# Two token tiles at a stage border: landing order, a two-engine evacuation and constant matmuls

## The chip, the cores and the metric

The kernel runs on one core of a Trainium2 chip. The metric is the device time of one execution in microseconds (us), lower is better. Each time is the median of several runs.

## What is computed

The program chains two blocks of two layers over 256 tokens of width 1024, in float32, and every layer is a mixer followed by a mixture of 16 experts. Between them stand residual additions and layer norms:

```python
h = _layer_norm(x) * (1.0 + sc1) + sh1
mix = _mixer(h, w_in[l], ...)
x = _layer_norm(DN_ALPHA * x + g1 * mix, ln1_g[l], ln1_b[l])
h = _layer_norm(x) * (1.0 + sc2) + sh2
ffn = _moe(h, w_router, router_bias, ...)
x = _layer_norm(DN_ALPHA * x + g2 * ffn, ln2_g[l], ln2_b[l])
```

That is a layer of the first block. In the second block the mixer is a gated linear attention in layer 0 and a differential attention in layer 1, there is no modulation by `sc` and `sh`, and each norm stands behind its addition in the same way.

## The kernel before

The 256 tokens are two token tiles of 128 rows, and both live in one SBUF tile `X` for the whole program. Every float32 product of the mixers is made from high and low parts: `hh` and `hl` of the activations, `whi` and `wlo` of the weights, with three matmuls for each pair (`acc<-whi,hh`, `acc<-whi,hl`, `acc<-wlo,hh`). The high part is a rounding to fp32r, and the low part is what is left of the value.

There are four mixtures in the order of the program, which the code tags `moe10`, `moe11`, `moe20` and `moe21`. This text calls them the first to the fourth. Their last step and the first step of what follows are what the text calls a **border**: border 1 leads from the first mixture into the mixer of layer 1 of the first block (`block1`, line 1116), border 2 from the second into the gated linear attention (`gla`, line 1506), border 3 from the third into the differential attention (`diff`, line 1683), and behind the fourth comes the end of the program (line 1858).

A mixture works through eight pairs of experts, `pi` 0 to 7. At its start the router (lines 541 and 567) makes the chosen experts' mask `r_m`. While PE waits for it, `keep_warm` (lines 702 and 946) issues matmuls of constants into a bank that nobody reads; their number is the third one in `WARM` (line 98). Then five small matmuls (line 704) make the places `pos` of the tokens, DVE turns them into one-hot rows `oh` (line 720), and the matmuls `pg` gather the tokens.

A pair ends with `spread`, which brings the experts' output `y` back to the token tiles (matmuls `sc`, one bank for each token tile and half of the columns), and `land`, which adds it to `X` (line 851). At the last pair `land` also does the norm that follows, through an object of the class `Tail` (line 255): `count` takes the statistics of one half (BN_STATS), `first` closes them (BN_AGGR, `ve` on DVE, then the power `rs` on POOL, line 189), and `affine` applies them in two passes, one with the mean (line 278) and one with `rs` (line 281). In the first block a second set of statistics follows for the norm of the next layer.

The next stage then transposes each token tile on PE (line 300), eight blocks of 128x128 into two banks `pt`, and evacuates them as `hh` and `hl`. At border 1 DVE first normalises (`z`, line 1208), and the evacuation also modulates. For each bank ACT makes three of four blocks and DVE the fourth in float32 (`hf`), then DVE casts all four to `hh` and subtracts for `hl`:

```python
if c < 3:
    S.activation(t[:, c], pt[:, c], AF.Identity, bias=sh1[:, k:k + 1], scale=sc1[:, k:k + 1])
else:
    V.tensor_scalar(t[:, c], pt[:, c], sc1[:, k:k + 1], sh1[:, k:k + 1], op0=OP.mult, op1=OP.add)
V.tensor_copy(hh[dst], t)
V.tensor_tensor(hl[dst], t, hh[dst].bitcast(F32), op=OP.subtract)
```

The order on each engine is settled when the program is built. Around a border (`chain_begins` to `chain_ends`, lines 235 to 249) the order of DVE, POOL, ACT and PE is the one in which the code was written; elsewhere a scheduler sets it. Each engine takes its instructions strictly in that order, and waits at the head of its row for the semaphores of the others.

Of the kernel before, what the change touches and what calls it, by code (L numbers as in the profile page):

```python
# [10 lines left out]
F32 = mybir.dt.float32  # L11
# [3 lines left out]
AF = mybir.ActivationFunctionType  # L15
# [81 lines left out]
TAIL_ENG = (ENG.Activation, ENG.PE)  # L97
WARM = ((3, 2, 6), (3, 2, 6))
LAM_WAIT = 8
# [26 lines left out]
def body(ctx: ExitStack, tc: tile.TileContext, A: dict, out: bass.AP, dbg=None):  # L126
# [135 lines left out]
    class Tail:  # L262
# [7 lines left out]
        def count(self, tt, h):  # L270
            self.stats[tt].add(h, X[:, tt, h * 512:(h + 1) * 512])

        def first(self, tt):
            self.mr[tt] = self.stats[tt].close()

        def affine(self, tt):
            x, (mu, rs) = X[:, tt], self.mr[tt]
            V.scalar_tensor_tensor(x, x, mu, self.rows[:, 0], op0=OP.subtract, op1=OP.mult)
            again = Stats(2)
            for h, hs in enumerate((slice(0, 512), slice(512, 1024))):  # L280
                V.scalar_tensor_tensor(x[:, hs], x[:, hs], rs, self.rows[:, 1, hs], op0=OP.mult, op1=OP.add)  # L281
                if self.again:
                    again.add(h, x[:, hs])
                yield hs
            if self.again:
                self.mr[tt] = again.close()
# [341 lines left out]
    def moe(z, kind, slots, scored, wg, wu, wd, mod, gate, tag, after, again, reorder=False, room=()):  # L628
# [7 lines left out]
        with ExitStack() as es:  # L636
# [167 lines left out]
            def down(pi, st, aT, last=False):  # L804
# [4 lines left out]
                for h in range(2):  # L809
# [19 lines left out]
                    if last and h == 0 and NF > 2:  # L829
                        land(pi, 0, spread(st, yh, yl, 0))  # L830
                if last and NF == 2:
                    land(pi, 0, sc)
                return yh, yl

            def spread(st, yh, yl, h):

                hs = slice(h * 512, (h + 1) * 512)
                scs = []
                for tt in range(2):
                    sc = ps.tile([P, 512], F32, tag="sc", name="sc", bufs=2)  # L840
                    mm3(sc, [(st[:, tt * P:(tt + 1) * P], yy[:, hs]) for yy in (yh, yl)])
                    scs.append(sc)
                return scs

            def land(pi, h, scs):
                hs = slice(h * 512, (h + 1) * 512)
                for tt, sc in enumerate(scs):
                    if pi == 0:
                        V.scalar_tensor_tensor(X[:, tt, hs], X[:, tt, hs], ALPHA, sc, op0=OP.mult, op1=OP.add)
                    else:  # L850
                        V.tensor_tensor(X[:, tt, hs], X[:, tt, hs], sc, op=OP.add)  # L851
                    if pi == 7 and (tt, h) != (1, 1):
                        tail.count(tt, h)
                    if pi == 7 and (tt, h) == (0, 1):
                        tail.first(0)
                        for _ in tail.affine(0):
                            pass

# [67 lines left out]
            for pi in range(8):  # L926
                if pi < 7:
                    if pi % 2 == 1:
                        gx = gather(pi // 2 + 1)
                    gu = up(pi + 1, gx[1])  # L930
                st = ga[0]
                ys = down(pi, *ga, pi == 7)
                if pi < 7:
                    ga = act(pi + 1, gx[0], gx[2], *gu)
                    land(pi, 0, spread(st, *ys, 0))
                land(pi, 1, spread(st, *ys, 1))
                if pi == OV_AT:
                    overflow()
                if pi == 6:
                    tail = Tail(after(), again)  # L940
                    chain_begins(*TAIL_ENG)
            rings[:] = [ring] * RING
            turn[0] = 0
# [172 lines left out]
    def block1(l, prev):  # L1116

        with tc.tile_pool(name="gp", bufs=1, reuse_waits="tile") as gp:
            gates[l, 1] = gp.tile([P, D], F32, name="g2")
            es = gp.tile([P, 2, NE], F32, name="es")  # L1120
            with ExitStack() as stack:
# [67 lines left out]
                def ev(tt, q, pt):  # L1189
                    ts = slice(tt * P, (tt + 1) * P)  # L1190
                    t = dl.tile([P, 4, P], F32, tag="hf", name="hf", bufs=2)
                    for c in range(4):
                        k = 4 * q + c
                        if c < 3:
                            S.activation(t[:, c], pt[:, c], AF.Identity, bias=sh1[:, k:k + 1], scale=sc1[:, k:k + 1])
                        else:
                            V.tensor_scalar(t[:, c], pt[:, c], sc1[:, k:k + 1], sh1[:, k:k + 1], op0=OP.mult, op1=OP.add)
                    dst = (slice(None), slice(4 * q, 4 * q + 4), ts)
                    V.tensor_copy(hh[dst], t)
                    V.tensor_tensor(hl[dst], t, hh[dst].bitcast(F32), op=OP.subtract)  # L1200

                if prev is not None:
                    for tt in range(2):
# [5 lines left out]
                        if tt == 0:  # L1209
                            prev.count(1, 1)  # L1210
                            prev.first(1)
                        prev.lows()
                        transposed(ps, "tp", z[:, tt], tt, ev)
                    chain_ends()
                dump(f"x{l}", X)
# [290 lines left out]
    def gla(prev, gp, room, load_router, logits, rows):  # L1506
        with tc.tile_pool(name="dl", bufs=1, reuse_waits="tile") as dl, tc.tile_pool(name="d", bufs=1, reuse_waits="tile") as d, tc.tile_pool(name="d2", bufs=2, reuse_waits="tile") as d2, \
# [21 lines left out]
            for tt in range(2):  # L1529
                if tt == 0:  # L1530
                    prev.count(1, 1)
                    prev.first(1)
                else:
# [149 lines left out]
    def diff(prev, gp, room, load_router, logits, rows):  # L1683
        with tc.tile_pool(name="dl", bufs=1, reuse_waits="tile") as dl, tc.tile_pool(name="d", bufs=1, reuse_waits="tile") as d, tc.tile_pool(name="d2", bufs=2, reuse_waits="tile") as d2, \
# [24 lines left out]
            for tt in range(2):  # L1709
                if tt == 0:  # L1710
                    prev.count(1, 1)
                    prev.first(1)
                else:
# [139 lines left out]
    ov = out[0].rearrange("(t p) d -> t p d", p=P)  # L1853
    prev.count(1, 1)
    prev.first(1)
    for tt in range(2):
# [40 lines left out]
```

## Time and profile before

| | us |
|---|---|
| median of three runs | 1644.25 (1643.98 to 1645.04) |
| profiled execution, its own time | 1644.99 |
| its span, from the first to the last instruction | 1643.2 |
| PE busy | 1464.9 (89%) |
| DVE busy | 867.5 (53%) |
| ACT busy | 430.3 (26%) |
| POOL busy | 132.9 (8%) |
| mean granted clock of PE | 0.952 of full speed |

A row of a timeline gives the start from the beginning of the span, the duration, the engine and line, the operation with the tile it writes and those it reads, and in square brackets how long the engine was idle before it and who released it. An `x8` behind a row says that eight instructions of one kind stand in it. A line number can be that of a helper. A matmul in float32 has two rows, one in fp32r has one. The granted clock is 1.00 at 2.4 GHz and 0.50 at 1.2 GHz.

### The profile page before, as it was taken

The page shows a single profiled execution, that of the slowest core. Times are in us where ns is not written, and L with a number is a line of the kernel's source. Part 1 is how long each engine was busy: PE and PEld are TensorE (multiplying, and loading weights), DVE is VectorE, ACT ScalarE, POOL GpSimd, SP SyncE. Part 2 cuts the span into 40 slices and gives each one's busy share as a digit, 9 for nine tenths or more (in the row PEclk, how much of TensorE's full clock was granted, in tenths as well). Part 3 has the DMA queues.
Part 4 walks back from the last instruction along what each step waited for, and adds up shares of the span by engine and source line. Part 5 has one row for each costly group of instructions (what it writes and reads, how often), then busy time and mean ns, then how long its engine had stood idle before and what let it go on. Part 6 is the DMA issues. An engine that isn't in the chain of part 4 may idle for free. (4 is left out here: it accounts for less than half of the span.)

```text
span 1643.2 us, 22584 instructions
## 1 busy us (share of the span) xinstructions
PE 1464.9 (89%) x9024; PEld 968.6 (59%) x9024; DVE 867.5 (53%) x1678; ACT 430.3 (26%) x729; POOL 132.9 (8%) x140
## 2 busy tenths in 40 slices
PE   4899997998699999599878998999898999999896
PEld 3788896443288899444447695443336988344332
DVE  3788898343798779524363574221126776122214
ACT  1453341111244433111125242010003552101000
POOL 0300002000130000200020001000002002000000
PEclk9999998999799999799989999999998999999898
DMA  9978699994775688899476387999989856999992
GB/s 307 365 245 282 202 312 352 340 308 165 248 252 171 205 294 251 240 367 358 156 241 199 104 290 256 375 376 366 360 306 296 272 204 240 359 367 387 334 387 104
DMA packets 324383, 461.80 MB, mean 281 GB/s; under 512 B 20077, under 2 KB 178285, under 8 KB 324258
## 3 DMA queue, kind: packets, MB, share of 16 engines
q1 hardware_dynamic: 308400, 445.29, 79.0%
q10 hardware_dynamic: 15858, 14.85, 3.5%
q8 instruction: 77, 1.26, 0.3%
q14 instruction: 48, 0.39, 0.1%
HBM read 456.43 MB, written 3.67 MB: 280 GB/s over the span
## 5 line engine op out<-in xcount | busy, mean ns | idle before, releaser
L763 PE MATMUL gu<-w,xg 128*64 128x512 f32 x1536 | 366.6, 597 | 7.3 <-ACT sa L796 6.5
L763 PEld LDWEIGHTS gu<-w,xg 128*64 128x64 f32 x1536 | 111.2, 137 | 218.9 <-issue 203.1
L817 PE MATMUL y<-w,sa 128*64 128x512 f32 x768 | 207.1, 596 | 1.1 <-DVE sa L801 1.1
L335 DVE TENSOR_TENSOR wlo<-w,whi 128x2048 fp32r<-128x2048 f32 (+2 forms) x92 | 183.4, 1997 | 45.3 <-ACT whi L325 42.4
L325 ACT ACTIVATE whi<-w 128x2048 fp32r<-128x2048 f32 (+2 forms) x92 | 157.7, 1726 | 141.0 <-PE acc L406 103.2
L828 DVE TENSOR_TENSOR yy<-y,yy 128x512 fp32r<-128x512 f32 x32 | 22.1, 692 | 197.3 <-ACT yy L827 197.3
L817 PEld LDWEIGHTS y<-w,sa 128*64 128x64 f32 x768 | 60.9, 137 | 107.4 <-issue 101.0
L501 DVE SCALAR_TENSOR_TENSOR adac<-w,ce,adac 128x512 f32<-128x512 f32 x140 | 104.5, 747 | 1.2
L313 PE MATMUL sc<-yy,st 128*128 128x512 f32 x256 | 87.2, 434 | 19.2 <-ACT yy L827 11.0
L313 PE MATMUL pg<-oh,zh 128*128 128x256 f32 x256 | 77.8, 332 | 25.3 <-DVEq L870 21.7
L406 PE MATMUL acc<-hh,whi 128*128 128x256 f32 x608 | 92.5, 294 | 1.7 <-ACT whi L325 1.7
L406 PE MATMUL acc<-hl,whi 128*128 128x256 f32 x608 | 93.0, 288 | 0.0
L827 ACT ACTIVATE yy<-y 128x512 fp32r<-128x512 f32 x32 | 19.1, 597 | 274.4 <-PE y L817 274.4
L406 PE MATMUL acc<-hh,wlo 128*128 128x256 f32 x608 | 87.1, 282 | 0.2 <-DVE wlo L335 0.2
L851 DVE TENSOR_TENSOR x<-x,sc 128x512 f32<-128x512 f32 x112 | 73.3, 681 | 22.0 <-PE sc L313 21.9
L406 PEld LDWEIGHTS acc<-hh,whi 128*128 128x128 f32 x608 | 80.0, 194 | 7.7 <-issue 4.7
L406 PEld LDWEIGHTS acc<-hl,whi 128*128 128x128 f32 x608 | 80.2, 191 | 4.8 <-issue 4.2
L313 PEld LDWEIGHTS pg<-oh,zh 128*128 128x128 f32 x256 | 58.3, 229 | 39.1 <-PEq L870 18.6
L189 POOL TENSOR_TENSOR rs<-ve,mhalf 128x1 f32<-128x1 f32 x24 | 25.3, 1055 | 678.7 <-DVE ve L188 678.7
L313 PEld LDWEIGHTS sc<-yy,st 128*128 128x128 f32 x256 | 42.0, 188 | 63.5 <-ACT yy L827 26.7
L406 PEld LDWEIGHTS acc<-hh,wlo 128*128 128x128 f32 x608 | 77.8, 188 | 2.2 <-issue 1.7
L823 DVE TENSOR_TENSOR yt<-y,g 128x512 f32<-128x512 f32 x32 | 22.0, 688 | 106.5 <-PE y L817 95.4
(375 smaller groups left out, 2196.9 us busy)
## 6 DMA issues: line engine op xcount, KB each, us to landing
w<-in_moe_w_gate_dram SPq DMA_DIRECT2D x64, 1024.0 KB, 12.1
w<-in_moe_w_up_dram SPq DMA_DIRECT2D x64, 1024.0 KB, 14.3
w<-in_moe_w_down_dram SPq DMA_DIRECT2D x128, 512.0 KB, 10.8
w<-in_w_ada_dram SPq DMA_DIRECT2D x47, 1024.0 KB, 6.5
w<-in_w_in_dram SPq DMA_DIRECT2D x40, 1024.0 KB, 6.6
w<-in_w_exp_gate_dram SPq DMA_DIRECT2D x64, 512.0 KB, 8.7
w<-in_w_exp_up_dram SPq DMA_DIRECT2D x64, 512.0 KB, 8.8
w<-in_w_exp_down_dram SPq DMA_DIRECT2D x64, 512.0 KB, 9.1
```

The source lines that it names most:

```text
L189: G.tensor_tensor(dst, ve, mhalf[:, :n], op=OP.pow)
L313: PE.matmul(dst, l, r, start=(i == 0), stop=(i == n - 1), skip_group_check=True)
L325: S.activation(hi[:, k0:k0 + n], w, AF.Copy)
L335: eng.tensor_tensor(lo[:, k0 + x:k0 + y], w[:, x:y], hi[:, k0 + x:k0 + y].bitcast(F32), op=OP.subtract)
L406: PE.matmul(dst, l, r, start=(start and i == 0), stop=(i == n - 1), skip_group_check=True)
L501: V.scalar_tensor_tensor(acc, ws[k // 4][:, k % 4], ce[:, k:k + 1], acc, op0=OP.mult, op1=OP.add)
L763: PE.matmul(gu[64 * j:64 * j + 64, :], xg[:, 4 * kh + k, (2 * pr + j) * CAP:(2 * pr + j + 1) * CAP], ws[j][:, k, :], start=(kh == 0 and k ...
L817: PE.matmul(y[64 * j:64 * j + 64, :], aT[:, f, 64 * j:64 * j + 64], w[:, j, k, :], start=(f == 0), stop=(f == NF - 1), tile_position=(0, 6 ...
L823: V.tensor_tensor(yt[:, hs], y, gate[:, hs], op=OP.mult)
L827: S.activation(yh[:, hs], src, AF.Copy)
L828: V.tensor_tensor(yl[:, hs], src, yh[:, hs].bitcast(F32), op=OP.subtract)
L851: V.tensor_tensor(X[:, tt, hs], X[:, tt, hs], sc, op=OP.add)
```

## The change

- `WARM`: 12 instead of 8 constant matmuls stand in front of `pos` at the start of each mixture.
- `TAIL_WARM` (new): behind the last `spread` of a mixture stand 14 constant matmuls at the first, 8 at the second and third, none at the fourth. At border 1 three more stand behind the transposes of each token tile.
- `land` is called for one token tile at a time. The first tile's halves land first, and its norm begins; the second tile's first half lands between the two passes of the first tile's `affine`, its second half behind it. `second` takes the statistics of both halves of the second tile, behind the work on the first. The last `spread` writes to banks of another tag (`gu`), so it need not wait for those of the first half.
- Border 1's evacuation: for each of four blocks ACT makes `hh` from `pt`, rounded as it is written, and DVE makes `hf` from the same `pt`. The cast is gone.

```diff
-WARM = ((3, 2, 6), (3, 2, 6))
+WARM = ((3, 2, 10), (3, 2, 10))
+TAIL_WARM = {"moe10": (14, 3), "moe11": (8, 0), "moe20": (8, 0), "moe21": (0, 0)}
...
+        def second(self):
+            for h in range(2):
+                self.count(1, h)
+            self.first(1)
...
-        def affine(self, tt):
+        def affine(self, tt, between=None):
             x, (mu, rs) = X[:, tt], self.mr[tt]
             V.scalar_tensor_tensor(x, x, mu, self.rows[:, 0], op0=OP.subtract, op1=OP.mult)
+            if between is not None:
+                between()
...
+                if last:
+                    if NF == 2:
+                        land(pi, 0, sc[:1])
+                    scs = spread(st, yh, yl, 1, "gu")
+                    land(pi, 1, scs[:1])
+                    tail.first(0)
+                    for _ in tail.affine(0, lambda: land(pi, 0, sc[1:], 1)):
+                        pass
+                    land(pi, 1, scs[1:], 1)
...
+            keep_warm(ps, "tp", 2, TAIL_WARM[tag][0])
...
-                        if c < 3:
-                            S.activation(t[:, c], pt[:, c], AF.Identity, bias=sh1[:, k:k + 1], scale=sc1[:, k:k + 1])
-                        else:
-                            V.tensor_scalar(t[:, c], pt[:, c], sc1[:, k:k + 1], sh1[:, k:k + 1], op0=OP.mult, op1=OP.add)
+                        S.activation(hh[:, k, ts], pt[:, c], AF.Identity, bias=sh1[:, k:k + 1], scale=sc1[:, k:k + 1])
+                        V.tensor_scalar(t[:, c], pt[:, c], sc1[:, k:k + 1], sh1[:, k:k + 1], op0=OP.mult, op1=OP.add)
                     dst = (slice(None), slice(4 * q, 4 * q + 4), ts)
-                    V.tensor_copy(hh[dst], t)
                     V.tensor_tensor(hl[dst], t, hh[dst].bitcast(F32), op=OP.subtract)
...
-                            prev.count(1, 1)
-                            prev.first(1)
+                            prev.second()
                         prev.lows()
                         transposed(ps, "tp", z[:, tt], tt, ev)
+                        keep_warm(ps, "acc", 3, TAIL_WARM["moe10"][1])
```

The same `prev.second()` stands in `gla`, `diff` and at the end of the program.

The first place is PE at border 1: `sc` is the last spread, `pt` the transposes (eight blocks for each token tile), `acc` the products of the mixer of layer 1, of which the first 48 read the first token tile. Before:

```order
L817 MATMUL y<-w,sa 64x512 x6
L313 MATMUL sc<-yy,st 128x512 x8
L300 MATMUL pt<-consts,z 128x128 x8
L406 MATMUL acc<-whi,hh 128x256 x8
L406 MATMUL acc<-whi,hl 128x256 x8
L406 MATMUL acc<-wlo,hh 128x256 x8
L406 MATMUL acc<-whi,hh 128x256 x8
L406 MATMUL acc<-whi,hl 128x256 x8
L300 MATMUL pt<-consts,z 128x128 x8
L406 MATMUL acc<-wlo,hh 128x256 x8
```

Now:

```order
L825 MATMUL y<-w,sa 64x512 x6
L321 MATMUL sc<-yy,st 128x512 x8
L964 MATMUL warm<-consts 128x256 x14
L308 MATMUL pt<-consts,z 128x128 x8
L964 MATMUL warm<-consts 128x256 x3
L308 MATMUL pt<-consts,z 128x128 x8
L964 MATMUL warm<-consts 128x256 x3
L414 MATMUL acc<-whi,hh 128x256 x8
L414 MATMUL acc<-whi,hl 128x256 x8
L414 MATMUL acc<-wlo,hh 128x256 x8
```

The transposes of the second token tile used to stand behind 40 of the 48 products on the first tile. Now no product stands between the transposes of the two tiles: all 48 follow the second tile's, with constant matmuls before each group.

The second place is ACT at border 1, with the engines whose semaphores each instruction waits for (`PE_49`, `DVE_49`); `pt` with four numbers are the four banks of the two token tiles. Before:

```order
L1195 ACTIVATE hf_5419<-pt_5414,modc_83 128x128 [waits PE_49]
L1195 ACTIVATE hf_5419<-pt_5414,modc_83 128x128 x2
L1195 ACTIVATE hf_5431<-pt_5426,modc_83 128x128 [waits PE_49]
L1195 ACTIVATE hf_5431<-pt_5426,modc_83 128x128 x2
L1195 ACTIVATE hf_5460<-pt_5455,modc_83 128x128 [waits DVE_49,PE_49,Activation_49]
L1195 ACTIVATE hf_5460<-pt_5455,modc_83 128x128 x2
L1195 ACTIVATE hf_5472<-pt_5467,modc_83 128x128 [waits DVE_49,PE_49,Activation_49]
L1195 ACTIVATE hf_5472<-pt_5467,modc_83 128x128 x2
```

Now:

```order
L1207 ACTIVATE hh_5404<-pt_5433,modc_83 128x128 [waits PE_49]
L1207 ACTIVATE hh_5404<-pt_5433,modc_83 128x128 [waits DVE_49] x3
L1207 ACTIVATE hh_5404<-pt_5448,modc_83 128x128 [waits PE_49]
L1207 ACTIVATE hh_5404<-pt_5448,modc_83 128x128 [waits DVE_49] x3
L1207 ACTIVATE hh_5404<-pt_5484,modc_83 128x128 [waits PE_49]
L1207 ACTIVATE hh_5404<-pt_5484,modc_83 128x128 [waits DVE_49] x3
L1207 ACTIVATE hh_5404<-pt_5499,modc_83 128x128 [waits PE_49]
L1207 ACTIVATE hh_5404<-pt_5499,modc_83 128x128 [waits DVE_49] x3
```

ACT used to make three blocks of a bank in a row, waiting once for PE. Now it waits for DVE before each block but the first of a bank, and DVE's four `hf` of a bank each wait for ACT.

The third place is DVE at the start of the third mixture, from `pm` to `oh`, which PE's `pg` waits for (`r_d` and `r_c` are the router's weights). The start of the fourth reads the same way. Before:

```order
L711 TENSOR_SCALAR pm<-r_m 128x32
L712 TENSOR_TENSOR pm<-pm,pos 128x32
L580 TENSOR_REDUCE r_gs_11914<-lg 128x2
L586 TENSOR_TENSOR r_c<-el,r_m 128x32
L720 TENSOR_TENSOR oh<-consts,pm 128x256 x2
L588 TENSOR_REDUCE r_d<-r_c 128x2
L921 COPY pos_sb<-pos 128x48
L589 TENSOR_TENSOR r_d<-r_d,r_gs_11914 128x2
L865 TENSOR_REDUCE cmax<-pos_sb 128x1
L590 RECIPROCAL r_d<-r_d 128x2
L867 CAST cnt<-cmax 128x1
L591 TENSOR_TENSOR r_c<-r_c,r_d 128x32
```

Now:

```order
L719 TENSOR_SCALAR pm<-r_m 128x32
L588 TENSOR_REDUCE r_gs_11970<-lg 128x2
L594 TENSOR_TENSOR r_c<-el,r_m 128x32
L596 TENSOR_REDUCE r_d<-r_c 128x2
L597 TENSOR_TENSOR r_d<-r_d,r_gs_11970 128x2
L598 RECIPROCAL r_d<-r_d 128x2
L599 TENSOR_TENSOR r_c<-r_c,r_d 128x32
L720 TENSOR_TENSOR pm<-pm,pos 128x32
L933 COPY pos_sb<-pos 128x48
L728 TENSOR_TENSOR oh<-consts,pm 128x256 x2
```

The four small operations of the router that stood behind `oh` (`r_d` twice, the reciprocal, `r_c`) and `pos_sb` now stand before it.

## Rows read from the trace of the kernel before

**Rows 1.** Page, part 1: busy time of each engine.

```profile
PE 1464.9 (89%) x9024; PEld 968.6 (59%) x9024; DVE 867.5 (53%) x1678; ACT 430.3 (26%) x729; POOL 132.9 (8%) x140
```

**Rows 2.** Waits of PE, whole span: total, times, longest.

```profile
PE pos L704 <- DVE r_m L537: 23.2, 4, 16.0
...
PE pt L300 <- DVE z L1208: 10.4, 3, 7.9
PE ptq L1291 <- DVE qro L1285: 7.2, 2, 4.5
```

**Rows 3.** Windows: busy time (instructions) by engine, granted clock, DMA share, GB/s.

```profile
278.80:281.20 2.40, 0.00 (x1) 0.00 (x0) 2.16 (x11) 0.00 (x0) 0.21 (x1) 1.00 1.04 394
281.46:288.30 6.84, 5.87 (x20) 4.05 (x20) 2.78 (x14) 1.13 (x2) 1.19 (x2) 0.50 1.08 364
435.06:452.10 17.04, 6.27 (x26) 5.61 (x27) 15.68 (x26) 4.94 (x8) 7.34 (x6) 0.50 0.45 141
672.90:688.90 16.00, 0.04 (x1) 0.00 (x0) 6.16 (x14) 2.40 (x6) 6.90 (x8) 0.64 0.94 309
1001.70:1008.50 6.80, 5.67 (x30) 5.58 (x31) 3.14 (x18) 0.60 (x1) 1.19 (x2) 0.50 0.91 339
1390.80:1394.20 3.40, 3.40 (x18) 3.40 (x17) 0.92 (x4) 0.60 (x1) 1.20 (x2) 0.50 1.05 389
496.60:499.90 3.30, 3.24 (x15) 3.25 (x16) 3.30 (x4) 1.20 (x2) 0.00 (x0) 0.50 0.00 0
```

**Rows 4.** Timeline, border 1, first token tile: start, us, engine, line, operation.

```profile
432.54 0.67 DVE L851 TENSOR_TENSOR x<-x,sc 128x512 f32<-128x512 f32 x1
...
437.32 0.75 DVE L281 SCALAR_TENSOR_TENSOR x<-x,rs,rows 128x512 f32<-128x512 f32 x1 [0.44 <-POOL rs L189]
...
441.28 1.00 DVE L1208 TENSOR_SCALAR z<-x,mv,rs 128x512 f32<-128x512 f32 x2
...
443.03 2.21 ACT L1195 ACTIVATE hf<-pt,modc 128x128 f32<-128x128 f32 x6 [5.24 <-PE pt L300]
...
444.23 0.41 DVE L1197 TENSOR_SCALAR hf<-pt,modc 128x128 f32<-128x128 f32 x1 [0.29 <-ACT hf L1195]
...
445.89 1.65 DVE L1200 TENSOR_TENSOR hl<-hf,hh 128x512 fp32r<-128x512 f32 x1
...
449.58 1.28 DVE L278 SCALAR_TENSOR_TENSOR x<-x,mv,rows 128x1024 f32<-128x1024 f32 x1
```

**Rows 5.** Timeline, border 1, second token tile.

```profile
457.72 1.34 DVE L335 TENSOR_TENSOR wlo<-w,whi 128x1024 fp32r<-128x1024 f32 x1
...
457.94 0.63 PE L300 MATMUL pt<-consts,z 128*128 128x128 f32 x4 [0.78 <-DVE z L1208]
...
460.99 1.73 PE L406 MATMUL acc<-whi,hh 128*128 128x256 f32 x8
...
461.39 0.69 DVE L1200 TENSOR_TENSOR hl<-hf,hh 128x512 fp32r<-128x512 f32 x1
...
463.49 1.07 PE L406 MATMUL acc<-wlo,hh 128*128 128x256 f32 x8
```

**Rows 6.** Timeline, start of the third mixture.

```profile
995.91 3.70 PE L951 MATMUL warm<-consts 128*128 128x256 f32 x16
...
1002.66 0.76 DVE L720 TENSOR_TENSOR oh<-consts,pm 128x256 fp32r<-128x256 f32 x2
...
1003.13 0.58 PE L313 MATMUL pg<-oh,zh 128*128 128x256 f32 x1 [0.81 <-DVE oh L720]
...
1003.33 0.18 DVE L588 TENSOR_REDUCE r_d<-r_c 128x2 f32<-128x32 f32 x1
```

**Rows 7.** Timeline, end of the program.

```profile
1626.16 0.70 DVE L199 BATCH_NORM_STATS2 s<-x 128x6 f32<-128x512 f32 x1
...
1633.63 1.42 DVE L281 SCALAR_TENSOR_TENSOR x<-x,rs,rows 128x512 f32<-128x512 f32 x2 [0.49 <-POOL rs L189]
```

**Rows 8.** Timeline of PE, border 2.

```profile
859.87 0.51 PE L406 MATMUL acc<-wlo,hh 128*128 128x256 f32 x2 [0.93 <-POOL wlo L335]
```

More of the change, by code (lines that the diff above doesn't have):

```diff
@@ L829, in down, with spread @@
                     if last and h == 0 and NF > 2:
-                        land(pi, 0, spread(st, yh, yl, 0))
-                if last and NF == 2:
-                    land(pi, 0, sc)
+                        sc = spread(st, yh, yl, 0)
+                        land(pi, 0, sc[:1])
+                if last:
+                    if NF == 2:
+                        land(pi, 0, sc[:1])
+                    scs = spread(st, yh, yl, 1, "gu")
[4 more added lines that the diff above has]
+                    land(pi, 1, scs[1:], 1)
                 return yh, yl
-            def spread(st, yh, yl, h):
+            def spread(st, yh, yl, h, bank="sc"):
                 hs = slice(h * 512, (h + 1) * 512)
@@ L839, in spread @@
                 for tt in range(2):
-                    sc = ps.tile([P, 512], F32, tag="sc", name="sc", bufs=2)
+                    sc = ps.tile([P, 512], F32, tag=bank, name="sc", bufs=2)
                     mm3(sc, [(st[:, tt * P:(tt + 1) * P], yy[:, hs]) for yy in (yh, yl)])
@@ L843, in spread, with land @@
                 return scs
-            def land(pi, h, scs):
+            def land(pi, h, scs, first=0):
                 hs = slice(h * 512, (h + 1) * 512)
-                for tt, sc in enumerate(scs):
+                for tt, sc in enumerate(scs, first):
                     if pi == 0:
@@ L851, in land @@
                         V.tensor_tensor(X[:, tt, hs], X[:, tt, hs], sc, op=OP.add)
-                    if pi == 7 and (tt, h) != (1, 1):
+                    if pi == 7 and tt == 0:
                         tail.count(tt, h)
[L854 to L857, printed above, removed]
             def overflow():
@@ L935, in moe @@
                     land(pi, 0, spread(st, *ys, 0))
-                land(pi, 1, spread(st, *ys, 1))
+                    land(pi, 1, spread(st, *ys, 1))
                 if pi == OV_AT:
@@ L1530, in gla @@
                 if tt == 0:
-                    prev.count(1, 1)
-                    prev.first(1)
+                    prev.second()
                 else:
@@ L1710, in diff @@
                 if tt == 0:
-                    prev.count(1, 1)
-                    prev.first(1)
+                    prev.second()
                 else:
@@ L1853, in body @@
     ov = out[0].rearrange("(t p) d -> t p d", p=P)
-    prev.count(1, 1)
-    prev.first(1)
+    prev.second()
     for tt in range(2):
```

## Prediction

> **What bounds the kernel now.** Read the busy times first: PE works in 89% of the span [rows 1], so time comes or goes where PE waits or its clock is low. The waits of PE come second. The change aims at two of them: the wait of `pos` for the router's `r_m` at the four starts of mixtures, and the wait of the transposes `pt` for `z` at border 1 [rows 2]. The windows come third, for the granted clock. After the wait of 2.40 us at the start of the first mixture PE works in 5.87 of the next 6.84 us, at 0.50 of its clock; the third start has 6.80 us at 0.50, the fourth 3.40, and border 1 has 17.04, of which PE works in 6.27 only [rows 3]. A stretch at half clock costs half of PE's work in it, where PE is what is waited for. At border 1 it is not: there the timeline shows one row of steps on DVE, POOL and ACT, for which PE waits [rows 4, 5].
>
> **The change part by part.** The sum is made against the profiled execution, 1644.99 us, which lies 0.74 above the median of the three runs, 1644.25; the working ends on the median. About 0.2% (3.3 us) is what a measurement of this kernel can tell from no change.
>
> *Four more constant matmuls at each start.* Sixteen rows of them take 3.70 us [rows 6], so eight rows more take 1.7 to 1.9. They lie wholly in waits of 2.4 us (first, third, fourth) and 16.0 us (second) [rows 3, 6], so `pos` is not late.
> - First start: the wait shrinks from 2.40 to about 0.6 us. If the clock then stays up, the 5.87 us at half clock take half: a gain of 2.9. If not, nothing. I take 2.9, since the clock was at 1.00 before that wait and at 0.50 behind it.
> - Second start: 14 us of the 16.0 remain [rows 3]. Nothing.
> - Third start: the same gain would be up to 2.8 (half of 5.67 [rows 3]). Against it stands the new order on DVE. `oh` is behind four small operations that each need the one before; one of them lasts 0.18 us [rows 6], about 0.2 with its handover, so `oh` and then `pg` come 0.8 later, and the wait between `pos` and `pg` grows from 0.81 [rows 6] to 1.6 us. That second wait can lower the clock for a part of what the first one no longer does. I take 0.8 lost and 0.8 gained, zero; the ends are -2.0 and +0.8.
> - Fourth start: the same 0.8 lost. The stretch at half clock is shorter, 3.40 us, so at most 1.7 comes back. The gap nearer to that stretch is the one that grows, so I take +0.7; the ends are -0.9 and +0.8.
>
> A rule of the Trainium skill speaks against the gain at the starts. In "TensorE: Matmul & The Clock Gate", section "Why this matters for your kernels", it asks for no idle gaps of PE above about 3 us between bursts of matmuls; a gap of 2.40 us would then not be what lowers the clock, and filling it would give nothing. The row disagrees: behind 2.40 us the granted clock is 0.50 [rows 3]. By the rule the sum would lose its 2.9.
>
> *Border 1, up to `z`.* Two steps of the second token tile leave the front of DVE's row: landing 0.67 and statistics 0.69 [rows 4, 7]. The landing comes back into the wait for POOL of 0.44 [rows 4] and sticks out by 0.2. So `z` starts 1.1 earlier, at 440.2 instead of 441.28. Statistics of two halves instead of one now stand behind `z` (+0.7), so DVE reaches its first `hf` at 443.4; before, it came at 444.23 [rows 4].
>
> *Border 1, the evacuation.* In the trace DVE's `hf` starts at 444.23, when the third of ACT's six has just ended: they start 0.35 apart and last 0.46, so the third ends at 443.03 + 0.70 + 0.46 = 444.19 [rows 4]. Two engines do not read one bank together there. In the new order each of four blocks is ACT, then DVE, then ACT, each waiting for the other: 0.46 + 0.41 and two handovers of 0.04, so 0.93 for a block. Of a bank, the last `hf` ends 3 x 0.93 + 0.41 = 3.2 after the first began. Then `hl` follows, 1.65 beside POOL for the first bank [rows 4] and 0.69 alone for the second [rows 5]. From 443.4 that gives 446.6, 448.2, 451.4 and 452.1. DVE begins the norm of the second tile at 452.0 instead of 449.58 [rows 4], 2.4 later. The cast that is saved does not pay for this.
>
> *Border 1, PE.* This is the largest term. Before, 40 products on the first tile ran while the second was normalised, and only eight were left. Now all 48 stand behind the second tile's transposes. The last of these begin at 457.94 [rows 5] + 2.4 = 460.3 and take about 0.4 in their spacing, three constant matmuls take 1.3 (six rows at about 0.22, from sixteen in 3.70 [rows 6]), and 48 products at full clock take 5.5 (eight end 1.07 after they start and start within 0.8 [rows 5]). The first product on the second tile then starts at 467.6; before it started at 460.99 [rows 5]. That is +6.6. The other row of steps is DVE's: `wlo` at 457.72 + 2.4 ends 461.4, then come twice 3.2 + 0.69 with a handover, and the last `hl` ends at about 469.1 instead of 462.1 [rows 5]: +7.0. The two agree, and I take +7.0. At half clock the 48 products take 5 more, which is the upper end, +11; the lower is +6.
>
> *Border 2.* `pt` comes 1.2 earlier, but PE then waits for `wlo` from POOL as before [rows 8], and POOL's part starts after the second tile's statistics, which are hardly earlier. Zero, with ends -0.5 and +0.5.
>
> *Border 3 and the end.* Here the half `h0` of the second tile was landed and counted in idle time of DVE (its statistics are the first row of [rows 7]); now it lands in POOL's wait of 0.49 [rows 7], 0.2 too long for it, and its statistics, 0.70, stand on the path; back to back some 0.3 of this overlaps. +0.6 at each.
>
> *What is hidden.* The 14 constant matmuls behind border 1's last spread take 28 x 0.21 = 5.9 us in the wait of 7.9 [rows 2]; the 8 at borders 2 and 3 take 3.4 in the waits for the first tile there. They end before `z` does. If they did not, `pt` would be late by the excess.
>
> **Sum:** -2.9 + 0 + 0 + 0.7 + 7.0 + 0 + 0.6 + 0.6 = **+6.0**, so 1650.2 on the median.
>
> **Rivals.**
> 1. *The loss at border 1 is absorbed later.* In the mixer that follows PE waits 4.5 us for the rotated queries `qro` [rows 2]. If PE came 7.0 later and DVE's part were not late too, that wait would vanish, and half of the 3.2 us that PE works at half clock behind it [rows 3] with it: 6.0 - 4.5 - 1.6 = -0.1, so 1644.2. With the clock gain of the third start as well (-2.0) it is 1642.2, and where the fourth start gains too (-1.6), 1640.6. This ends on the side of not slower. For it: the wait is there. Against it: DVE stands 7 us late itself at 469, and `qro` comes from DVE. It decides from 3 us of absorption on.
> 2. *Reading one bank by two engines overlaps after all.* Then a block costs about 0.4 and DVE begins the second tile's norm at 448.9, 0.7 earlier than before. The 48 products still follow the transposes: 457.94 - 0.7 + 0.4 + 1.3 + 5.5 = 464.4, so border 1 is left with +3.4 and the sum is +2.4, 1646.6. The Trainium skill excludes it ("PSUM — Partial Sum Buffer", section "PSUM bank collisions raise a hardware error": two engines on one bank are to be ordered by semaphores); the waits in the new order and 444.23 [rows 4] say the same.
> 3. *The first start does not recover*, because the clock falls in what is left of the two waits around `pos`: no -2.9, so 1653.1. The rule on gaps cited above would come to the same time.
>
> **How the numbers follow.** The forecast itself has 0.60, of which 0.05 lies within the bound; rival 1 has 0.22 (0.10 faster by over 0.2%, 0.12 within), rival 2 has 0.05, rival 3 has 0.13. So faster 0.10, same 0.22, slower 0.68. The likeliest case by itself reaches from 1647 to 1653. The range goes from 1644.0, which leaves out half of rival 1, to 1655.5, which takes in rival 3 and about half a stretch of half clock at border 1.
>
> **What would show it.** In the changed trace `z` of border 1 starts about 1 us earlier; ACT's `hh` and DVE's `hf` alternate in steps of 0.93; PE has no products between the transposes of the two tiles; the first product on the second tile comes some 7 us later in relation to the last `sc`; the wait of PE for `qro` is still over 3 us; the first mixture's `pg` run at full clock. The forecast is wrong if the alternation is quicker than 0.8 a block, if the `qro` wait vanishes, or if the third and fourth starts come out at full clock throughout.

## The result and the profile after

| | before | changed |
|---|---|---|
| median of 14 runs each, us | 1644.94 | 1653.73 |
| lowest to highest, us | 1643.14 to 1651.04 | 1650.45 to 1664.78 |
| ratio, 95% interval | | 1.0057 (1.0040 to 1.0073) |
| span of the profiled execution, us | 1643.2 | 1648.7 |
| mean granted clock of PE | 0.952 | 0.961 |

The changed kernel is slower by 0.57%, 9.4 us of 1645 (6.6 to 12.0). The mean clock went up, and so did the time. The profiled execution of the change took 1650.45 us by itself, which is the fastest of its 14 runs; its trace shows 5.5 us of the difference.

The page of the changed kernel begins so:

```profile
span 1648.7 us, 22786 instructions
...
PE 1483.9 (90%) x9128; PEld 981.1 (60%) x9128; DVE 870.3 (53%) x1686; ACT 432.8 (26%) x733; POOL 130.8 (8%) x140
```

The waits of PE in the changed kernel (total, times, longest):

```profile
PE pos L712 <- DVE r_m L545: 19.5, 4, 15.8
...
PE pt L308 <- DVE z L1218: 16.4, 3, 13.9
...
PE pg L321 <- DVE oh L728: 5.0, 4, 1.6
```

Before, the third row read:

```profile
PE pg L313 <- DVE oh L720: 3.6, 4, 1.0
```

The wait for `r_m` went from 23.2 to 19.5 and the one of `pt` for `z` from 10.4 to 16.4 [rows 2]: a border that was to be shortened got a longer wait. The wait of `pg` for `oh` went from 3.6 to 5.0; its longest was 1.0 and is 1.6 now.

The windows at half clock in the changed kernel, in the columns of [rows 3]:

```profile
279.90:282.30 2.40, 0.03 (x2) 0.01 (x1) 2.16 (x11) 0.00 (x0) 0.19 (x1) 1.00 1.06 398
283.10:286.60 3.50, 3.07 (x14) 3.10 (x15) 1.25 (x8) 0.56 (x1) 1.19 (x2) 0.51 1.06 370
447.00:464.00 17.00, 6.09 (x22) 5.15 (x23) 12.86 (x20) 3.55 (x8) 6.04 (x9) 0.50 0.35 110
501.60:505.00 3.40, 2.99 (x14) 3.02 (x15) 3.37 (x4) 0.60 (x2) 0.00 (x0) 0.50 0.37 124
1027.20:1030.70 3.50, 3.50 (x12) 1.20 (x12) 0.69 (x1) 0.00 (x0) 0.00 (x0) 0.51 1.05 389
1392.50:1395.90 3.40, 3.00 (x14) 3.00 (x15) 1.43 (x5) 0.60 (x1) 1.30 (x2) 0.50 1.04 392
1416.40:1419.80 3.40, 3.40 (x12) 1.22 (x12) 0.69 (x1) 0.00 (x0) 0.00 (x0) 0.50 1.05 389
```

The start of the first mixture has one stretch of 3.4 us at half clock instead of 6.84, the third start has none. But border 1 has 17 us as before, and two stretches are new, 1027.2 and 1416.4, some 25 us into the third and fourth mixtures.

Setting each instruction's start in the changed trace against its start before gives the difference place by place. The first 1.1 us arise before the first start, in code that the change does not touch; in the profiles of the experiments this place lies between -1.5 and +3.5.

| place | forecast | in the profiles |
|---|---|---|
| beginning of the program | 0 | +1.1 |
| start of the first mixture | -2.9 | -1.3 |
| further on in the first mixture | 0 | -0.7 |
| border 1, to the first products on the second tile | +7.0 | +8.0 |
| from there to behind the rotated queries | 0 | -1.3 |
| second mixture, its start included | 0 | -0.4 |
| border 2 and the products behind it | 0 | -4.4 |
| third mixture, its start included | 0 | +0.6 |
| border 3 | +0.6 | +0.4 |
| fourth mixture, its start included | +0.7 | +3.0 |
| end | +0.6 | +0.5 |
| sum | +6.0 | +5.5 |

**Border 1** in the changed kernel, first token tile (timeline):

```profile
439.10 1.00 DVE L1218 TENSOR_SCALAR z<-x,mv,rs 128x512 f32<-128x512 f32 x2
...
442.26 0.40 DVE L1208 TENSOR_SCALAR hf<-pt,modc 128x128 f32<-128x128 f32 x1
442.70 0.46 ACT L1207 ACTIVATE hh<-pt,modc 128x128 fp32r<-128x128 f32 x1 [1.77 <-DVE hf L1208]
...
443.19 0.41 DVE L1208 TENSOR_SCALAR hf<-pt,modc 128x128 f32<-128x128 f32 x1 [0.53 <-ACT hh L1207]
443.64 0.46 ACT L1207 ACTIVATE hh<-pt,modc 128x128 fp32r<-128x128 f32 x1 [0.48 <-DVE hf L1208]
444.13 0.41 DVE L1208 TENSOR_SCALAR hf<-pt,modc 128x128 f32<-128x128 f32 x1 [0.53 <-ACT hh L1207]
...
445.51 1.46 DVE L1210 TENSOR_TENSOR hl<-hf,hh 128x512 fp32r<-128x512 f32 x1
...
450.76 1.28 DVE L284 SCALAR_TENSOR_TENSOR x<-x,mv,rows 128x1024 f32<-128x1024 f32 x1
```

Two engines take turns: DVE's `hf` starts at 442.26, ACT's `hh` at 442.70, DVE's at 443.19, each 0.03 to 0.04 after the other has ended, and a pair takes 0.94 us. `z` starts 9.42 us after DVE's last `yy`, against 10.67 before. The norm of the second tile starts 21.08 us after it, against 18.97 [rows 4].

The second token tile (timeline):

```profile
459.03 1.11 PE L308 MATMUL pt<-consts,z 128*128 128x128 f32 x4 [0.29 <-DVE z L1218]
...
459.93 2.77 PE L964 MATMUL warm<-consts 128*128 128x256 f32 x6
...
462.14 2.17 PE L414 MATMUL acc<-whi,hh 128*128 128x256 f32 x8
...
467.27 0.69 DVE L1210 TENSOR_TENSOR hl<-hf,hh 128x512 fp32r<-128x512 f32 x1
...
468.69 1.07 PE L414 MATMUL acc<-whi,hh 128*128 128x256 f32 x8
```

The three constant matmuls (six rows) take 2.8 us, since the clock is at half until 464.0; the first eight of the 48 products take 2.17 instead of 1.07. The first product on the second tile starts at 468.69.

### The profile page after: what moved, and what is told of

Its sections match the earlier page's. It is cut to its first block, busy times and chain, and to the rows that moved or that the text cites. A ratio compares the mean times of both kernels' runs of the same rounds, so it can differ in the third digit from the quotient of the medians.

```text
span 1648.7 us, 22786 instructions
## 1 busy us (share of the span) xinstructions
PE 1483.9 (90%) x9128; PEld 981.1 (60%) x9128; DVE 870.3 (53%) x1686; ACT 432.8 (26%) x733; POOL 130.8 (8%) x140
## 5 line engine op out<-in xcount | busy, mean ns | idle before, releaser
L343 DVE TENSOR_TENSOR wlo<-w,whi 128x2048 fp32r<-128x2048 f32 (+2 forms) x92 | 183.4, 1998 | 41.8 <-ACT whi L333 38.8
L321 PE MATMUL pg<-oh,zh 128*128 128x256 f32 x256 | 74.1, 322 | 28.1 <-DVEq L882 21.6
L867 DVE TENSOR_TENSOR x<-x,sc 128x512 f32<-128x512 f32 x112 | 73.5, 682 | 23.9 <-PE sc L321 23.8
## 6 DMA issues: line engine op xcount, KB each, us to landing
w<-in_moe_w_down_dram SPq DMA_DIRECT2D x128, 512.0 KB, 10.7
```

Source lines behind the costliest of these rows:

```text
L321: PE.matmul(dst, l, r, start=(i == 0), stop=(i == n - 1), skip_group_check=True)
L343: eng.tensor_tensor(lo[:, k0 + x:k0 + y], w[:, x:y], hi[:, k0 + x:k0 + y].bitcast(F32), op=OP.subtract)
```

## The experiments

Most of these are told by a mark inside the trace, since it is free of what happens elsewhere: the time from DVE's last `yy` of the first mixture to the first `acc<-whi,hl` on the second tile. Beside it stand the end of the last `hl` and the first transpose `ptq` of the rotated queries, from the same `yy`. The ratio is the whole time against runs of the kernel before from the same rounds. The change has 14 runs, e1, e2, e4 and e5 have 6 each, the others 10 to 12.

| kernel | product | last `hl` | `ptq` | median, us | ratio (95%) |
|---|---|---|---|---|---|
| before | 32.0 | 31.5 | 66.1 | 1644.9 | |
| the change | 39.9 | 38.3 | 70.6 | 1653.7 | 1.0057 (1.0040 to 1.0073) |
| e1, without the three | 38.0 | 38.8 | 74.7 | 1656.9 | 1.0070 (1.0054 to 1.0085) |
| e2, old evacuation | 37.0 | 30.6 | 67.7 | 1654.3 | 1.0063 (1.0047 to 1.0079) |
| e3, both undone | 30.6 | 30.7 | 65.1 | 1647.4 | 1.0017 (1.0000 to 1.0034) |
| e4, longer rows at starts alone | 32.0 | 31.5 | 66.2 | 1649.9 | 1.0023 (1.0008 to 1.0038) |
| e5, new evacuation alone | 38.7 | 39.5 | 75.0 | 1654.7 | 1.0057 (1.0036 to 1.0079) |
| e6, the three alone | 37.3 | 31.5 | 68.0 | 1647.7 | 1.0018 (1.0000 to 1.0036) |
| e7, e1 with parted loops | 29.2 | 31.2 | 65.8 | 1644.9 | 0.9998 (0.9979 to 1.0016) |
| e8, landing order alone | 30.6 | 30.7 | 65.1 | 1646.0 | 1.0007 (0.9990 to 1.0024) |
| e9, e7 without longer rows | 29.2 | 31.2 | 65.7 | 1646.2 | 1.0008 (0.9996 to 1.0021) |
| e10, landing order and parted loops | 29.2 | 31.2 | 65.7 | 1646.0 | 1.0005 (0.9994 to 1.0016) |
| e11, e7 with longer rows at two starts | 29.3 | 31.2 | 65.8 | 1645.4 | 0.9995 (0.9980 to 1.0009) |
| e12, 14, 8 and 8 alone | 31.9 | 31.3 | 66.0 | 1645.4 | 1.0009 (0.9996 to 1.0023) |

**e1: without the three constant matmuls at border 1.**

```diff
-TAIL_WARM = {"moe10": (14, 3), ...
+TAIL_WARM = {"moe10": (14, 0), ...
```

> The changed kernel without the three constant matmuls behind each token tile's transposes at border 1, everything else as changed. They share the banks of the mixer's products, so without them the 40 products on the first tile stand ahead of the second tile's transposes again. Measure: from DVE's last yy of the first mixture to the first acc<-whi,hl on the second tile, 32.0 us before (430.61 to 462.56) and 39.9 in the change (429.68 to 469.59). Theory (two rows of steps end together, the order on PE and the alternation of ACT and DVE, and undoing one leaves the other): DVE and ACT still finish the second tile some 6 us later than before, so 36 to 38, and the whole is 2 to 4 us faster than the change. Rival A (the order on PE alone): 31 to 33, the whole 7 to 9 faster than the change. Rival B (the alternation alone): 39 to 41, the whole as the change.

The mark came at 38.0, at the upper end of the theory; both rivals fall. PE's 40 products are back ahead of the second tile's transposes, and DVE ends the second tile as late as in the change, 38.8. The whole did not gain, though 2 to 4 us were expected: at the queries this kernel is 4 us behind the change, 74.7 against 70.6.

**e2: the evacuation of before, the rest as changed.**

```diff
-                        S.activation(hh[:, k, ts], pt[:, c], AF.Identity, ...)
-                        V.tensor_scalar(t[:, c], pt[:, c], ...)
+                        if c < 3:
+                            S.activation(t[:, c], pt[:, c], AF.Identity, ...)
+                        else:
+                            V.tensor_scalar(t[:, c], pt[:, c], ...)
...
+                    V.tensor_copy(hh[dst], t)
```

> The changed kernel with the evacuation of before at border 1 (ACT three blocks, DVE one, then the cast), and the constant matmuls left in, so PE's order stays as changed. Same measure. Theory: the second tile's transposes come about 2.5 us earlier than in the change, the 48 products still follow them: 35 to 37, and the whole is 3 to 5 us faster than the change. Rival A (order alone): 39 to 41, the whole as the change. Rival B (alternation alone): 31 to 33, the whole 7 to 9 faster than the change.

The mark came at 37.0, the theory's upper end, while `hl` ends at 30.6: here PE's order alone holds the products back. The whole is no better than the change's, against the expectation. In its profile it stands 2.4 us above before behind border 1 and 2.3 below behind border 2. From there to the end it loses 10.7 us, 9.8 of them in the third and fourth mixtures, where its code is the change's.

**e3: both undone.** The two diffs above together.

> Both undone at border 1: no three constant matmuls and the evacuation of before, while the landing order, the 14 and 8 constant matmuls and the longer row at the starts stay. Same measure. Theory and both rivals: 30 to 32, the whole 7 to 9 us faster than the change. What is open is the rest: if the terms outside border 1 sum to -2.5 as in the profile of the change (first start -1.3, border 2 -4.4, the others +3), the whole is 2 to 3 us faster than before; if they sum to zero or more, it is no faster than before.

The mark came at 30.6, and the whole is 6.3 us faster than the change by the medians (7 to 9 were expected). So the two parts together make up the loss at border 1, and what is left of the change is 0 to 0.34% slower than before, not shown to be faster.

**e4: the longer rows at the starts alone.**

```diff
-WARM = ((3, 2, 6), (3, 2, 6))
+WARM = ((3, 2, 10), (3, 2, 10))
```

> The kernel before with 12 instead of 8 constant matmuls at the starts of the mixtures and nothing else. The new order of DVE at the third and fourth starts comes with it. My forecast for these terms was -2.9, 0, 0 and +0.7, together -2.2. In the profile of the change they are -1.3 at the first, 0 at the second, and at the third and fourth +0.2 and +2.1 with the stretch at half clock that each has 25 us later: together about +1. Theory (the profile of the change): within 2 us of before. Rival (the forecast): 2 us faster. Rival (the clock gains all of its half stretches): 5 us faster.

It is 1.3 to 6.2 us slower. That excludes both rivals; the theory, within 2 us, is touched only by the lower end. Its profile is 3.8 us longer, of which 3.1 come before 90 us, where the two programs are the same; at the four starts together it is 0.7. Since leaving the longer rows out of the later versions gained nothing (e7 against e9), this loss is not shown to be theirs.

**e5: the new evacuation alone, on the kernel before.** The diff of e2 with its signs exchanged.

> The kernel before with border 1's new evacuation alone (ACT makes hh, DVE makes hf, block by block); landing, constant matmuls and PE's order as before. Measure as in the first four runs, from the last yy to the first acc<-whi,hl on the second tile (32.0 before, 39.9 in the change, 38.0 without the three, 37.0 with the old evacuation, 30.6 with both undone). Theory (each of the two parts costs 5 to 7 us here by itself, and together they cost little more than one): 37.5 to 39.5, and 6 to 9 us slower than before as a whole. Rival (the alternation costs only in company of the new landing order, which puts statistics ahead of it): below 35.

38.7, as the theory said, and about as slow as the whole change. The alternation needs no company. PE's waits show where it goes: the products now wait 7.4 us for ACT's `hh` (before, 3.9 for DVE's), and the wait for the rotated queries is as long as before (7.2 [rows 2]), so it takes nothing back:

```profile
PE acc L406 <- ACT hh L1194: 7.4, 11, 1.8
PE ptq L1288 <- DVE qro L1282: 7.4, 2, 4.7
```

**e6: the three constant matmuls alone, on the kernel before.**

```diff
                         transposed(ps, "tp", z[:, tt], tt, ev)
+                        keep_warm(ps, "acc", 3, 3)
```

> The kernel before with three constant matmuls behind each token tile's transposes at border 1, in the banks of the products, and nothing else. Same measure. Theory: all 48 products of the first tile move behind the second tile's transposes, 457.94 + 0.6 + 1.3 + 5.5 gives 465.4 for the first product on the second tile and 35.5 to 37.5 for the measure (up to 40 if they run at half clock); as a whole 3 to 6 us slower than before. Rival (constant matmuls raise the clock in the wait and pay for themselves): 31 to 33, no slower.

The mark is at 37.3, in the theory's range: with three constant matmuls in the ring of the products' banks all 48 products stand behind them, and PE waits 10.9 us in one piece for the second tile. That it is the shared ring, and not their place in the code, is read from the program; no run put them into other banks.

```profile
PE pt L300 <- DVE z L1208: 19.1, 3, 10.9
```

The whole lost 0 to 0.36%, that is 3.0 us (0 to 5.9), where the theory had 3 to 6. Of the 5.4 us at the mark 2.0 are left at `ptq`: here the wait for the queries does absorb, as rival 1 had it, because DVE is not late (31.5).

**e7: the loops parted, without the three.**

```diff
                         S.activation(hh[:, k, ts], pt[:, c], AF.Identity, ...)
+                    for c in range(4):
+                        k = 4 * q + c
                         V.tensor_scalar(t[:, c], pt[:, c], ...)
```

> The change without the three constant matmuls, and with the evacuation's loops parted: ACT makes the four blocks of a bank, then DVE makes its four hf of that bank, while ACT is in the next bank. The same instructions as in the change, one handover for a bank instead of seven. Same measure. Theory (the alternation is what costs, not the larger share of DVE): a bank costs DVE 4 x 0.33 to 0.41 for hf and 0.69 for hl, 2.0 to 2.4, against 3.9 in the change: 31 to 34, as a whole as with both undone (within 3 us of before). Rival (reading PSUM in float32 twice is what costs): 37 to 39, as a whole 6 to 12 us slower than before.

The same 32 instructions as in the change, in another order on the engines, and the border is shorter than before. The timeline of its first token tile:

```profile
444.05 2.91 ACT L1207 ACTIVATE hh<-pt,modc 128x128 fp32r<-128x128 f32 x8 [5.21 <-PE pt L308]
...
445.92 1.36 DVE L1210 TENSOR_SCALAR hf<-pt,modc 128x128 f32<-128x128 f32 x4
...
447.32 0.88 DVE L1212 TENSOR_TENSOR hl<-hf,hh 128x512 fp32r<-128x512 f32 x1
448.12 1.35 DVE L1210 TENSOR_SCALAR hf<-pt,modc 128x128 f32<-128x128 f32 x4
...
449.51 1.60 DVE L1212 TENSOR_TENSOR hl<-hf,hh 128x512 fp32r<-128x512 f32 x1
...
451.03 1.27 DVE L284 SCALAR_TENSOR_TENSOR x<-x,mv,rows 128x1024 f32<-128x1024 f32 x1
```

ACT makes eight blocks in 2.91 us without a break, DVE four in 1.36, and the norm of the second tile begins 17.7 us after the last `yy`, against 21.1 in the change and 19.0 before. The mark, 29.2, below the theory's 31 to 34, flatters this kernel a little, since the first half of `hl` suffices for that product; the last `hl` ends at 31.2, 0.3 earlier than before. At `ptq` these 0.3 are left, and the whole is as before, 12.0 us less than e1 by the medians, which differs from it in nothing but the order of the two loops.

**e8: the landing order alone.** The change with its three tables of constant matmuls set back and the evacuation of before.

> The kernel before with the landing order alone: first tile first, statistics of the second tile behind it, the last spread in the other banks; no added constant matmuls, old evacuation. Same measure. Theory: z 1.1 to 1.4 earlier, so 30.5 to 31; border 2 gains 1.2, border 3 and the end lose 0.4 and 0.5: 1 to 2 us faster than before in the sum of these. Rival (what DVE saves ahead of z is lost behind it, in the statistics of two halves): 31.5 to 32.5, and 1 us slower than before.

The mark is at 30.6 as expected. At border 2 the first transposes start 6.3 us after the last `yy` instead of 8.8, in every kernel with the new order and in none with the old one, but in e8 the 49th product behind them comes only 0.1 earlier than before (21.3 against 21.4). The end loses 0.5. The whole is the same as before; the 1 to 2 us that were expected are not seen.

**e9, e10 and e11: which constant matmuls the parted version needs.** All three are e7; e9 has `WARM` as before, e10 has no added constant matmuls at all, e11 has the longer rows at the first two starts only.

> The parted evacuation (as in the run before: ACT's four blocks of a bank, then DVE's four), the landing order and the 14 and 8 constant matmuls, without the three and without the longer rows at the starts. With the longer rows this took as long as before (ratio 0.9998). Theory (the longer rows cost 3 to 4 us, as alone, by the new order of DVE at the third and fourth starts and by clock stretches): 1640 to 1642, 2 to 4 us faster than before. Rival (the longer rows are worth nothing either way, their loss alone was chance of the clock): 1643 to 1646.

> The landing order and the parted evacuation alone, no added constant matmuls. Measure from the last yy to the first acc<-whi,hl on the second tile: 29 to 31, as with them, since PE's clock does not bind there. Theory (the landing order is worth nothing in sum, the parted evacuation gains 1.3 at border 1 that the wait for the rotated queries takes back): 1643 to 1646, within 0.2% of before. Rival (constant matmuls at the borders were what the parted version gained by): 1647 to 1649.

> As the first of this set, with the longer rows at the first and second starts alone, where DVE's order is that of before. Theory (their cost comes from DVE's order at the third and fourth): as without any, within 1 us. Rival (it comes from the rows themselves): 2 us or more slower than without any.

By their medians all three are within 0.2% of before and of each other. The theory of e9 (2 to 4 us faster) falls, that of e10 holds. e11 is not told apart from e9, so its question stays open, but it has no price worth asking for.

**e12: the constant matmuls behind the last spreads alone, on the kernel before.**

```diff
+            keep_warm(ps, "tp", 2, {"moe10": 14, "moe11": 8, "moe20": 8, "moe21": 0}[tag])
```

> The kernel before with the 14, 8 and 8 constant matmuls behind the last spreads alone. Theory (PE waits there for DVE and POOL, and what its clock gains in the products behind is waited for again at POOL's wlo): within 1.5 us of before; at border 1 the measure stays at 31.5 to 32.2. Rival (the clock that they hold up gains what the half stretches cost PE there): 3 us or more faster.

The theory holds: mark 31.9, whole as before. No version is shown to be faster than the kernel before.

## Why the prediction was right, and where it was wrong

The direction and the range held: 1653.7 in a range of 1644.0 to 1655.5, and slower. The size was low, +6.0 against +9.4 (6.6 to 12.0). The direction was right for its reason, the loss at border 1. That the profile's sum, +5.5, comes so near to +6.0 is luck: border 2 (-4.4) makes up for what border 1, the first start and the fourth mixture cost beyond the forecast, 1.0, 1.6 and 2.3.

**Border 1, right in both its parts.** The forecast had a pair of blocks at 0.93 us, and it took 0.94; the norm of the second tile 2.4 later, and it was 2.1; the last `hl` 7.0 later, and it was 6.8. That neither part is the cause alone was said in the forecast only as "the two agree"; e1, e2, e5 and e6 show it, since each part by itself costs 5 to 7 us at the mark. Further on they are not alike. From the last `yy` to the first `pos` of the second mixture the kernel before takes 258.3 us; the alternation without the three takes 10.2 and 9.8 more (e1, e5), the three without the alternation 3.8 and 3.3 (e2, e6), the change with both 6.7, and every other version between 0.9 less and 0.2 more. So the alternation is the dearer part, and in its company the three constant matmuls save 3.5 us there, by one profile each, instead of costing time. Low was the other row of steps: the forecast took the three constant matmuls and 48 products at full clock, +6.6, and named half clock as the upper end, +11. Half clock lasted to 464.0, into the eighth of these products, and the first product on the second tile came 8.6 later.

**The first start was mis-sized**: -2.9 forecast, -1.3 in the profile of the change. The step that failed is "Sixteen rows of them take 3.70 us [rows 6], so eight rows more take 1.7 to 1.9 [...] the wait shrinks from 2.40 to about 0.6". That row is the third start's. At the first start the sixteen rows of before took 5.39 us, because a part of them ran at half clock, and the change's twenty-four took 5.43 at full clock. Before (the clock was 0.51 from 274.6 to 278.1):

```profile
273.42 5.39 PE L951 MATMUL warm<-consts 128*128 128x256 f32 x16
```

In the change:

```profile
274.49 5.43 PE L964 MATMUL warm<-consts 128*128 128x256 f32 x24
282.28 0.17 PE L712 MATMUL pos<-r_m,tri 128*128 128x16 bf16 x1 [2.37 <-DVE r_m L545]
...
283.53 0.55 PE L321 MATMUL pg<-oh,zh 128*128 128x256 f32 x1 [0.98 <-DVE oh L728]
```

The wait is 2.37, as long as before. The eight rows were sized rightly, and the wait that they were taken from was not: with sixteen rows at full clock it is 4.08 to 4.09, in all six other profiles that have them at this start. In e8:

```profile
273.50 3.70 PE L964 MATMUL warm<-consts 128*128 128x256 f32 x16
281.28 0.17 PE L712 MATMUL pos<-r_m,tri 128*128 128x16 bf16 x1 [4.08 <-DVE r_m L545]
```

Only in e2, where the clock was low in these rows as well, did they reach as far as the forecast had it:

```profile
275.02 7.11 PE L964 MATMUL warm<-consts 128*128 128x256 f32 x24
282.81 0.17 PE L712 MATMUL pos<-r_m,tri 128*128 128x16 bf16 x1 [0.69 <-DVE r_m L545]
...
284.06 0.36 PE L321 MATMUL pg<-oh,zh 128*128 128x256 f32 x1 [0.98 <-DVE oh L728]
```

There `pg` ran at full clock and 2.6 us were gained. In e1, e3, e4, e7 and e11, with the same longer row, it was 0 to 0.2 lost: rival 3 in five of seven profiles. And e6, with the row of before, gained 1.2 there, with one stretch of 3.4 us at half clock like the change. So not even the change's -1.3 is shown to come from the longer row.

**The wait for the rotated queries.** The forecast said it would stay over 3 us. In the change it is 1.63 and 1.03:

```profile
496.02 2.30 DVE L343 TENSOR_TENSOR wlo<-w,whi 128x2048 fp32r<-128x2048 f32 x1
...
500.32 0.42 PEld L1301 LDWEIGHTS ptq<-consts,qro 128*128 128x128 f32 x4 [1.83 <-DVE g L523]
500.32 0.66 PE L1301 MATMUL ptq<-consts,qro 128*128 128x128 f32 x4 [1.63 <-DVE g L523]
...
502.01 1.09 PE L1301 MATMUL ptq<-consts,qro 128*128 128x128 f32 x4 [1.03 <-DVE qro L1295]
```

Of the 8.0 us at border 1, 4.6 are left at `ptq`, and behind it 2.1 are lost again, so that 6.7 stay. In e1 the wait is as long as before:

```profile
505.18 0.72 PEld L1301 LDWEIGHTS ptq<-consts,qro 128*128 128x128 f32 x4 [4.90 <-DVE qro L1295]
505.18 1.12 PE L1301 MATMUL ptq<-consts,qro 128*128 128x128 f32 x4 [4.70 <-DVE qro L1295]
```

The step that failed is the objection to rival 1, "DVE stands 7 us late itself": it is late, but the three constant matmuls also changed the order that the scheduler gave DVE and PE further on. In the change a `wlo` of 2.30 us stands at 496.02, in the wait for POOL's `rq`; in e1, as before, it stands ahead of the sum for that `rq`, which therefore starts later. In e2 and e6, which have the three, it stands as in the change. I did not read that part of the order before forecasting. So rival 1 had a share, though not the one that decides.

**Border 2** was forecast at zero and is -4.4 in the profiles. A part of it is not the change's: e4 and e6, with the code of before at that border, show -3.0 and -2.8 there against the same trace of before, which has a stretch of half clock at 882.2 to 885.6; e5, with the same code and such a stretch, shows -0.9. The versions with the new landing order show -2.7 (e8, without constant matmuls) to -4.7 (e7). How much of this the landing order and the eight constant matmuls earn is not settled.

**The third and fourth starts.** `oh` is late as forecast (`pg` waits 1.6 us). At the third start the whole stretch at half clock vanished, -1.4 net, and 25 us later a new one took 1.6 back. At the fourth, the sum of 0.7 came to 0.5 at the start and 1.6 at such a later stretch. These later stretches are not shown to come from the longer rows: at the third start e9, e10, e11 and e12 have one too, with the row of before, and e3 and e4, with the longer row, have none.

**Rivals 2 and 3, and the rest.** Rival 2 fell: 442.26 to 444.13 shows strict turns. Border 3 and the end came to +0.4 and +0.5 against +0.6 each. What is not settled is why the medians of the change and of e2 lie as high as they do. The profile of e1 is 11.1 us longer than that of before, of which border 1 explains 10.2. That of the change is 5.5 longer, and it is its fastest run. The one of e2 is 8.4 longer, with 3.8 at border 1 and 9.8 in the third and fourth mixtures; the change, with the same code there, loses 3.6. In these two mixtures, from the first `pos` to the last `yy`, the clock is at half for 41.0 us in e2, 23.9 in the change and 27.0 before. The 17.1 us between e2 and the change are enough for their difference of 6.2, since PE loses up to half of such time, but no run shows that they are its cause.

## What to carry to other kernels

Before two engines share a PSUM tile, read in the built order how often each waits for the other: DVE's four instructions on a bank took 3.2 us in turns with ACT and 1.4 when each engine did its four in one go, with the same work. A filler can move other instructions: three constant matmuls, alone (e6), put all 48 products of a tile behind a wait that 40 of them used to fill. And a row that is to fill a wait must be timed at that wait, at the clock that it has there, and the wait in more than one profile: the first start's was 2.40 us in one and 4.1 in six others.

## What the runs showed of the hardware

The clock fell behind waits of 2.4 us and 1.0 us, one close behind the other. In the change PE waits 2.37 us at 1.00, makes the five small `pos`, waits 0.98 and runs at 0.51 from 283.1; in the kernel before the waits are 2.40 and 0.97, and 0.50 follows [rows 3]. No run has the first of the two alone. The Trainium skill ("TensorE: Matmul & The Clock Gate", section "Why this matters for your kernels") asks for no idle gaps above about 3 us between bursts of matmuls; here the clock fell behind shorter ones too.

And the same wait of PE is sometimes followed by half clock and sometimes not. Some 25 us into the third mixture PE waits 2.52 us for ACT in both kernels, and the program is the same there. Before (timeline of PE):

```profile
1026.35 1.07 PE L763 MATMUL gu<-w,xg 128*64 128x512 f32 x2 [2.52 <-ACT sa L796]
```

The granted clock stayed at 1.00 behind it. In the change:

```profile
1025.92 1.07 PE L771 MATMUL gu<-w,xg 128*64 128x512 f32 x2 [2.52 <-ACT sa L804]
...
1027.72 3.81 PE L771 MATMUL gu<-w,xg 128*64 128x512 f32 x10
```

Here it fell to 0.51 from 1027.2 to 1030.7, and the ten `gu` in that row take 3.81 us, against 2.37 for ten before. Such stretches moved a place where nothing was changed: at the fourth start e12, with the code of before, lost 3.3 us against the profile of before. The runs of one kernel spread by 5.5 to 18 us (e5: 1652.1 to 1657.6 in 6 runs; e3: 1639.6 to 1657.7 in 12), and one profile is not enough to price a term of 2 us; a mark between two instructions of one border repeated to 0.1 us (30.6 in e3 and e8; 29.2 in e7, e9, e10, 29.3 in e11).
